# A two-layer hybrid trunk: conv taps split between TensorE and VectorE, a new split of the start's sums and dots, a packed dt product

## Chip, cores and metric

One core of one Trainium2 chip. The time is the device time of one execution in microseconds (us); the kernel's time is the median of several runs.

## What is computed

The reference is a two-layer trunk on x of shape (1, 512, 1024) in f32, conditioned by a vector c. Each layer is a mixer and a gated feed-forward network (FFN), each behind an RMSNorm with a shift and a scale that come from c. Cut to what the change touches:

```python
silu_c = silu(c)
for i in range(2):
    sh_m, sc_m, g_m, sh_f, sc_f, g_f = split(silu_c @ w_mod[i] + b_mod[i], 6)
    h = rmsnorm(x, norm_mix[i]) * (1 + sc_m) + sh_m
    y = even_mixer(h) if i == 0 else ssd_mixer(h)
    x = x + g_m * y
    h = rmsnorm(x, norm_ffn[i]) * (1 + sc_f) + sh_f
    x = x + g_f * conv_ffn(h)
return rmsnorm(x, final_norm)

# even_mixer: attention beside a conformer branch
a, g = split(conf_in, 2)                    # 512 channels each
h = causal_dwconv(a * sigmoid(g), conv_w, conv_b)   # 31 taps, per channel
h = silu(layernorm(h))
# ssd_mixer: z, xbc, dt = split(h @ w_in); dt has 32 columns
dt = softplus(dt + dt_bias)
```

## The kernel before, in words

Channels lie on the 128 partitions, tokens (512) along the free axis. Everything is in the function `trunk`: `even_layer` is layer 0's mixer, `odd_layer` layer 1's, `ffn` is called for both layers. The weights come from HBM in tiles of 128x1024 on SyncE's queue (L304); ScalarE rounds each tile to its high part (L312), VectorE takes the low part (L317), and a product is three matmuls per tile of 128 rows (`mm3`: L365 high by high, L366 high weight by low data, L367 low weight by high data).

The order of the work is made by a list-scheduling planner (`Plan`). A task has an engine, a cost, the tasks that it needs and the buffers that it takes and gives back; at each step the planner takes the ready task of the highest rank, and a table of numbers (MIXER0 for layer 0's mixer, MIXER1 for layer 1's) adds to the ranks. The order on TensorE (PE), ScalarE (ACT), VectorE (DVE) and GpSimd (POOL) is what the planner emits. SIDE tasks are the DMAs on GpSimd's queue, DMA tasks those on SyncE's (SP).

**Start.** x is loaded in eight tiles of 128 channels. ACT squares each (L672), PE sums the squares over the channels by matmuls against a vector of ones (L679: four 128x1 matmuls a tile, 32 in all). `warm` (L651) issues matmuls whose result is not used: two of 256 columns ahead of the sums, two behind them, three behind the spread of the norm factor. The shift and the scale of each 128 channels are dot products of silu(c) with 1024 weights, on DVE (`mod_dot`, L571: 128x1024, one for the scale and one for the shift of each of eight tiles kt). With them a tile's normalised data are split into high and low (L741, L745, L749), and TensorE adds this tile's part to six PSUM tiles at once (L753): the six first column blocks, which are the conv branch's a and g for three channel tiles. `finish` makes their last part with L365 to L367.

**Conv.** For each of four channel tiles i: ACT's sigmoid (L865), DVE's gate (L869, the result is `us[i]`), a store to an HBM row buffer with 30 zeros ahead (L872, on GpSimd's queue), and four fetches (L886, on GpSimd's queue, 270 KB each) that bring 32 channels each with four shifts, one in each block of 32 partitions. DVE makes the diagonal tap matrices (L877). `conv_product` (L893) runs 8 steps of 4 taps with 32 output channels per matmul: 32 matmuls a channel tile, 128 in all (31 taps, the 32nd is zero). ACT adds the bias from PSUM (L898), and PE forms the layer norm's mean (L1119) from the four results.

**dt.** In the odd layer `dt_in` makes the 32 dt columns by `mm3` (24 matmuls with 32 output rows), ACT copies them, and four transposes (L1393) turn them to tokens.

Of the kernel before, what the change touches and what calls it, by code (L numbers as in the profile page):

```python
# [21 lines left out]
ALU = mybir.AluOpType  # L22
# [12 lines left out]
CTAPS, CQ = 4, 8  # L35
# [4 lines left out]
_VEC = [("bmod", 96), ("nmix", 16), ("nffn", 16), ("fnorm", 8), ("bin", 14), ("ccw", 128), ("eye", 32),  # L40
# [29 lines left out]
WARM = (2, 2, 3)  # L70
# [3 lines left out]
MIXER1 = {'xdt': 122, 'differ': 108, 'square': 109, 'y_h': 85, 'join': 108, 'c4': 150, 'load': 91, 'weigh': -66, 'residual': -66, 'sums': -89, 'in': -132, 'osq': 53, 'head': 31, 'decay': 57, 'tokens': 114, 'state_in': -136, 'gate': 80, 'bt': -29, 'rows': 52, 'square_add': -7, 'root': 1, 'c4silu': 4, 'cbm': 34, 'newton': 45, 'out': -40, 'fetch': 95, 'c4tap': 135, 'yt': -82, 'pairs': -93, 'off': -50, 'turn': 75, 'rest': -66, 'skip': 99, 'osq_add': 62, 'diag': -21, 'dt': 123, 'norm': 0, 'z': -111, 'y_l': -149, 'carried': 11, 'free': -21, 'fetch_e': -26, 'grow': -23, 'state': 114, 'scan 2': -50, 'out 2': -150, 'scan 1': 76, 'in 2': -16, 'in 3': 2, 'in 0': 15, 'scan 3': -61, 'in 1': -150, 'out 3': -6, 'scan 0': 150, 'out 0': -35, 'out 1': -146, 'scr': 18}  # L74
N_XS, N_M, N_E = 8, 2, 2
N_S = 26
MIXER0 = {'sigmoid': 15, 'square': -70, 'osq_add': 86, 'head': -45, 'tap0': -113, 'attn_h': -71, 'conv_h': -27, 'out_c': -40, 'gated': 150, 'rest': -137, 'values': -27, 'rope': 53, 'rstd': -97, 'mod_sum': 7, 'attn_l': 150, 'var': -22, 'turn': 88, 'mod_end': 26, 'exp': 1, 'bring': 62, 'conv_sum': 54, 'out_a': 82, 'osq': -46, 'mod_act': -104, 'mod_add': 39, 'mod_free': 120, 'normalize': 121, 'load': -111, 'product': -139, 'mean_row': -71, 'mod_dve': 105, 'tap': -30, 'recip': 112, 'ln': 150, 'centre': -43, 'residual': -146, 'maxima': 21, 'rstd_row': -129, 'conv_l': 77, 'mean': 47, 'rope_in': 71, 'v_bias': -85, 'mod_load': -125, 'mod_dot': -93, 'root': 30, 'rows': 93, 'rows_in': 1, 'v_turn': -35, 'v_in': 112, 'mod 2': -75, 'head 0': 122, 'mu': 0, 'keys': 80, 'conv 0': 87, 'head 1': 90, 'mod 1': -108, 'head 3': -8, 'shifts': 58, 'scores': -52, 'mod 0': -50, 'conv 3': -51, 'conv 2': 119, 'cbias': 86, 'conv': 83, 'store': -26, 'taps': 96, 'conv 1': 150, 'head 2': 19, 'wg_load': -29, 'c_row': 8, 'norm': 51, 'hl': 8, 'x_newton': 150, 'preload': 31, 'others': -49, 'wg_head': 6, 'finish': 39, 'sines': 34, 'v_load': 121, 'first 4': 119, 'upper': 9, 'wg_rest': -15, 'hh': 130, 's_gain': -108, 'first 2': 100, 'widen': 150, 'x_load': -105, 'x_root': 57, 'x_add': -93, 'x_total': -33, 's_dot': 50, 'lh': 13, 'x_sq': -105, 'masks': -88, 't_turn': 29, 'c_in': -115, 'ss_load': -6, 'first 5': -3, 'gain': 23, 'w_free': -15, 'normed': 130, 'margins': -107, 'side': -45, 'x_row': -13, 'first 0': 29, 'h_dot': 103, 't_in': 26, 'first 1': -51, 'first 6': 29, 'angles': -108, 'first 3': 40, 'lower': 98, 'first 7': 52, 'h_bias': -80, 'x_sum': 24}
# [145 lines left out]
def trunk(ctx: ExitStack, tc: tile.TileContext, xT_d, vecs_d, rows_d, dsk_d, pos_d, const_d, wss_d, wg0_d,  # L223
# [397 lines left out]
    def even_layer(lp, cp, dp0):  # L621
# [26 lines left out]
        def warm(n):  # L648

            for _ in range(n):  # L650
                mm(g0[NG0 - 1][:, 0:2 * P], lhsT=ident, rhs=con[:, :2 * P], start=True, stop=True)  # L651
# [21 lines left out]

        def x_sum(k):
            if k == 0:
                st["xt"] = bank((P, NCH))
                warm(WARM[0])
# [3 lines left out]
            if k == KT - 1:  # L681
                warm(WARM[1])

        sums = None
        for k in range(KT):
            t = add("x_sq", "ACT", 0.62, lambda k=k: x_square(k), [xs_[k]], dict(tmp=1))
            sums = add("x_sum", "PE", 0.9, lambda k=k: x_sum(k), [t, sums, *cbs], dict(ps=1) if k == 0 else None, dict(tmp=1))
# [16 lines left out]
        def x_row():  # L704
            st["rb"] = spread(st["xr"])
            warm(WARM[2])
# [3 lines left out]
        rb_ = add("x_row", "PE", 2.1, x_row, [t], dict(ps=1))  # L710
# [24 lines left out]
        def shift(kt):  # L735
            S = modv[:, 0, kt:kt + 1]
            act(S, S, AF.Identity, bias=bm[:, 0, kt:kt + 1])
# [136 lines left out]
        def conv_taps(i):  # L874

            t_ = mod_raw().rearrange("p (n c) -> p n c", c=32)
            tt(t_, vec("eye", 0, 32).unsqueeze(1).broadcast_to([P, 32, 32]),  # L877
               vec("ccw", 32 * i, 32).unsqueeze(2).broadcast_to([P, 32, 32]), ALU.mult)
            st["cw", i] = t_.rearrange("p (g q) c -> p g q c", g=4)

        def conv_fetch(i):
# [3 lines left out]
            for g in range(4):  # L885
                nc.gpsimd.dma_start(u4[g], bass.AP(src.tensor, src.offset + 32 * g * CROW,  # L886
# [15 lines left out]
        def conv_tasks(i, after, pa, pg):  # L902
# [3 lines left out]
            d_ = plan.add("taps", "DVE", 1.3, lambda: conv_taps(i), [a_], dict(mr=1))  # L906
            c_ = plan.add("store", "SIDE", 1.0, lambda: conv_store(i), [b_])
            c_ = plan.add("shifts", "SIDE", 3.6, lambda: conv_fetch(i), [c_, margins_], dict(u4=1))
            c_ = plan.add("conv", "PE", 7.4, lambda: conv_product(i), [c_, d_], dict(ps=1), dict(mr=1, u4=1))
            conv_done[i] = plan.add("cbias", "ACT", 0.69, lambda: conv_bias(i), [c_], None, dict(ps=1))  # L910
# [423 lines left out]
    def odd_layer(lp, dp, start, after):  # L1334
# [17 lines left out]
        dwh, dwl = tmp((P, KT, 32), F32R), tmp((P, KT, 32), F32R)  # L1352
        split(wraw, dwh, dwl)
# [27 lines left out]
        def dt_in():  # L1381
            st["dtf"] = bank()
            for kt in range(KT):
                mm3(st["dtf"][0:32, :], (dwh[:, kt, :], dwl[:, kt, :]), *hn[kt], kt == 0, kt == KT - 1)

        def dt_copy():
            st["dts"] = tmp()
            nc.scalar.copy(st["dts"][0:32, :], st["dtf"][0:32, :])
# [58 lines left out]
        t = plan.add("dt", "PE", 5.2, dt_in, [], dict(ps=1))  # L1447
# [349 lines left out]
def pack(i):  # L1797
# [22 lines left out]
    r["wss"] = np.stack([wm[0][1], wm[0][0]], axis=1)  # L1820
    r["wmod"] = np.concatenate([wm[w // 6][w % 6] for w in MOD_ORDER])
# [15 lines left out]
    for g in range(4):  # L1837
# [6 lines left out]
    cw = np.zeros((CTAPS * CQ, 512), np.float32)  # L1844
    cw[:31] = a["conf_conv_w"][0]
# [4 lines left out]
        "ccw": cw.reshape(CQ, CTAPS, 4, 4, 32).transpose(1, 4, 2, 3, 0).reshape(P, P),  # L1850
# [37 lines left out]
```

## Time and profile before

| What | us |
|---|---|
| Median of three runs | 1365.77 (1363.56 to 1369.64) |
| Profiled execution, own time | 1364.35 |
| Its span in the trace | 1362.5 |
| PE busy | 1335.4 (98%) |
| DVE busy | 852.4 (63%) |
| ACT busy | 590.5 (43%) |
| POOL busy | 95.7 (7%) |

The profiled execution stands 1.42 us under the median. Its stages, in us from the start of the span: the start up to 57 (where `finish` begins), the products for the fourth channel tile up to 72, the conv from 72.05 to 118.4, attention and the mixer's output to about 238, FFN 0 to 620, the odd layer to 980, FFN 1 to 1340, the last norm to 1362.5. The busy share of TensorE is high in all of them, so the views that matter are the ones by stage.

### The profile page before, as it was taken

The numbers are of one execution on the slowest core, as the hardware profiler recorded it, in microseconds if no ns is written. First come the engines' busy times: TensorE is split into PE (matmuls) and PEld (weight loads), VectorE is DVE, ScalarE is ACT, GpSimd is POOL, SyncE is SP. The second block draws the span as 40 slices with busy tenths as digits, with TensorE's granted clock in tenths as the row PEclk, the third lists the DMA queues.
The fourth block names the chain that finished last, engine by engine and source line by source line (L and its number), as shares of the span: only waits on it lengthen the run. The fifth ranks groups of instructions, "written<-read, shape, count | busy, mean of one in ns | idle before, by whom it ended". The sixth has DMA issues, their size and how long they took to land.

```text
span 1362.5 us, 17553 instructions
## 1 busy us (share of the span) xinstructions
PE 1335.4 (98%) x6878; PEld 1093.9 (80%) x6879; DVE 852.4 (63%) x1316; ACT 590.5 (43%) x938; POOL 95.7 (7%) x173
## 2 busy tenths in 40 slices
PE   8979999999999999999999999999999999999997
PEld 7726778988888888898887887878898888888886
DVE  5912898786576567667588684788665434444443
ACT  4512763543233223246686762765354313322333
POOL 5420110000000000010010100110000000000001
PEclk7989999999999999999999999999999999999998
DMA  9595453475565565322552432432223233223311
GB/s 333 194 191 129 138 194 118 140 232 172 183 210 168 183 214 191 105 89 67 153 169 79 156 93 80 139 126 79 76 78 111 90 100 107 92 89 108 100 55 63
DMA packets 58212, 183.71 MB, mean 135 GB/s; under 512 B 10064, under 2 KB 13200, under 8 KB 58128
## 3 DMA queue, kind: packets, MB, share of 16 engines
q1 hardware_dynamic: 45184, 152.24, 35.2%
q0 software_dynamic: 12256, 29.69, 7.5%
q8 instruction: 54, 0.88, 0.3%
q10 hardware_dynamic: 688, 0.66, 0.2%
q14 instruction: 30, 0.25, 0.1%
HBM read 179.26 MB, written 3.28 MB: 134 GB/s over the span
## 4 chain that ended last, share of the span: by engine, by line
PE 87%; DMA 4%; DVE 3%; issue 2%; ACT 2%; POOL 1%; DVEq 0%; ACTq 0%; POOLq 0%
PE ps L365 26%; PE ps L367 26%; PE ps L366 26%; DMA s<-uc 2%; PE ps L893 2%; DMA M<-scr 2%; PE ps L399 1%; PE ps L391 1%; PE ps L1573 1%; PE ps L679 1%; ACT M L1523 1%; PE ps L1565 1%; PE ps L1551 1%; DVE mr L571 1%; PE ps L1041 0%
## 5 line engine op out<-in xcount | busy, mean ns | idle before, releaser
L365 PE MATMUL ps<-hn,wh 128*128 128x512 f32 (+1 forms) x1214 | 460.1, 379 | 0.8 <-ACT hn L441 0.8
L366 PE MATMUL ps<-hn,wh 128*128 128x512 f32 (+1 forms) x1214 | 454.1, 374 | 0.4
L367 PE MATMUL ps<-hn,wl 128*128 128x512 f32 (+1 forms) x1214 | 454.0, 374 | 0.0
L317 DVE TENSOR_TENSOR wl<-raw,wh 128x1024 fp32r<-128x1024 f32 (+1 forms) x208 | 250.8, 1209 | 144.4 <-ACT wh L312 143.4
L312 ACT CAST wh<-raw 128x1024 fp32r<-128x1024 f32 (+1 forms) x208 | 213.1, 1028 | 219.2 <-PE ps L366 209.9
L365 PEld LDWEIGHTS ps<-hn,wh 128*128 128x128 f32 x1214 | 228.6, 188 | 43.0 <-issue 1.7
L366 PEld LDWEIGHTS ps<-hn,wh 128*128 128x128 f32 x1214 | 228.7, 188 | 42.0 <-issue 1.4
L367 PEld LDWEIGHTS ps<-hn,wl 128*128 128x128 f32 x1214 | 228.5, 188 | 41.0
L454 DVE SCALAR_TENSOR_TENSOR x<-ps,modv,x 128x512 f32<-128x512 f32 (+1 forms) x108 | 73.7, 689 | 119.6 <-PE ps L367 119.4
L365 PE MATMUL ps<-fh,wh 128*128 128x512 f32 (+1 forms) x380 | 142.2, 374 | 0.0
L366 PE MATMUL ps<-fl,wh 128*128 128x512 f32 (+1 forms) x380 | 141.9, 373 | 0.0
L367 PE MATMUL ps<-fh,wl 128*128 128x512 f32 (+1 forms) x380 | 141.9, 373 | 0.0
L571 DVE SCALAR_TENSOR_TENSOR mr<-mr,cb 128x1024 f32<-128x1024 f32 x96 | 116.1, 1218 | 3.5 <-DMA mr<-in_wss_dram 2.2
L1281 ACT ACTIVATE tmp<-ps,vecs 128x512 f32<-128x512 f32 x44 | 34.3, 780 | 115.4 <-PE ps L367 115.4
L1282 DVE SCALAR_TENSOR_TENSOR tmp<-ps,vecs,tmp 128x511 f32<-128x511 f32 x44 | 32.9, 748 | 80.0 <-ACT tmp L1281 80.0
L366 PEld LDWEIGHTS ps<-fl,wh 128*128 128x128 f32 x380 | 71.5, 188 | 12.8
L365 PEld LDWEIGHTS ps<-fh,wh 128*128 128x128 f32 x380 | 71.5, 188 | 12.6
L367 PEld LDWEIGHTS ps<-fh,wl 128*128 128x128 f32 x380 | 71.5, 188 | 12.6
L429 POOL TENSOR_TENSOR ssq<-ssq,tmp 128x512 f32<-128x512 f32 x10 | 13.4, 1338 | 805.1 <-ACT tmp L428 805.1
L290 ACT CAST fh<-tmp 128x512 fp32r<-128x512 f32 x44 | 27.3, 620 | 96.4 <-DVE tmp L1286 96.4
L1284 ACT ACTIVATE tmp<-tmp 128x512 f32<-128x512 f32 x44 | 27.8, 633 | 74.9 <-DVE tmp L1283 74.9
L291 DVE TENSOR_TENSOR fl<-tmp,fh 128x512 fp32r<-128x512 f32 x44 | 30.5, 693 | 30.2 <-ACT fh L290 30.2
(277 smaller groups left out, 1500.0 us busy)
## 6 DMA issues: line engine op xcount, KB each, us to landing
raw<-in_w_dram SPq DMA_DIRECT2D x176, 512.0 KB, 3.7
mr<-in_wmod_dram SPq DMA_DIRECT2D x56, 512.0 KB, 3.6
raw<-in_w_dram SPq DMA_DIRECT2D x32, 448.0 KB, 3.3
mr<-in_wmod_dram POOLq DMA_DIRECT2D x24, 512.0 KB, 5.1
mr<-in_wss_dram SPq DMA_DIRECT2D x16, 512.0 KB, 6.2
M<-scr POOLq DMA_DIRECT2D x16, 512.0 KB, 4.7
s<-uc POOLq DMA_DIRECT2D x16, 270.0 KB, 15.1
raw<-in_wg_dram SPq DMA_DIRECT2D x8, 384.0 KB, 5.7
```

The lines of the kernel that those rows point to most:

```text
L290: nc.scalar.copy(h, src)
L291: (eng or nc.vector).tensor_tensor(l, src, h.bitcast(F32), ALU.subtract)
L312: nc.scalar.copy(h, self.raw[i].rearrange("p (k m) -> p k m", m=P))
L317: eng.tensor_tensor(l, self.raw[i].rearrange("p (k m) -> p k m", m=P), h.bitcast(F32), ALU.subtract)
L365: mm(ps, lhsT=w[0], rhs=ah, start=first, stop=False)
L366: mm(ps, lhsT=w[0], rhs=al, start=False, stop=False)
L367: mm(ps, lhsT=w[1], rhs=ah, start=False, stop=last)
L454: stt(x[:, m, hs], ps, gate(m), x[:, m, hs], ALU.mult, ALU.add)
L571: stt(raw, raw, 1.0, mod_pool[2], ALU.mult, ALU.mult, accum_out=out)
L1281: act(c, pg, AF.Identity, bias=vec("fcb", i), scale=vec("fcw", 3 * i + 2))
L1282: stt(c[:, 1:], pg[:, :T - 1], vec("fcw", 3 * i + 1), c[:, 1:], ALU.mult, ALU.add)
L1284: act(c, c, AF.Silu)
```

## The change

- **Square sums.** DVE adds the squares of tiles 1 to 5 onto tile 0's (`x_add`, five operations); PE sums that one, tile 6 and tile 7 (12 matmuls of 128x1 instead of 32).
- **Fillers.** The 256-column fillers at three fixed places become 16 tasks of one 128-column matmul each, which the planner places.
- **Shift dots.** For kt below 4 the shift's dot is made on PE (`pe_dot`: 8 f32 matmuls of 32x128 in four column groups; ACT copies the 128x128 result, `pe_in`; one matmul adds its rows, `pe_sum`). The host lays these weights out by row. DVE keeps the other four shift dots and all eight scale dots.
- **Conv.** PE makes 24 taps (CQ 8 to 6; 24 matmuls a channel tile). The last seven taps are made from `us[i]` directly: ACT makes the first with the bias (`late_first`, in place of the bias from PSUM), DVE the other six (`late_tap`, 128x506 to 128x511), and DVE adds the PSUM result (`conv_sum`). The fetches go to SyncE's queue.
- **dt.** The high and the low weights lie side by side, so that one matmul with 64 output rows makes high by high and low by high: 16 matmuls instead of 24. The four transposes become four matmuls against an identity of two blocks, which adds the halves.
- **Order.** MIXER0 and MIXER1 have new numbers.

```diff
-CTAPS, CQ = 4, 8
+CTAPS, CQ = 4, 6
+NLATE = 31 - CTAPS * CQ
-WARM = (2, 2, 3)
+WARM = 16
+PE_DOTS = 4
-MIXER0 = {'sigmoid': 15, 'square': -70, ...}
+MIXER0 = {'sigmoid': 33, 'square': -70, ...}
...
-                mm(g0[NG0 - 1][:, 0:2 * P], lhsT=ident, rhs=con[:, :2 * P], start=True, stop=True)
+            mm(g0[NG0 - 1][:, 0:P], lhsT=ident, rhs=con[:, :P], start=True, stop=True)
...
+        def x_add(k):
+            tt(st["xq", 0], st["xq", 0], st["xq", k], ALU.add)
...
+            elif k < KT - 2:
+                sums = add("x_add", "DVE", 0.69, lambda k=k: x_add(k), [t, sums], None, dict(tmp=1))
...
+        def pe_dot(kt):
+            o = st["pd", kt] = bank((P, 2 * P))
+            for n in range(0, KT, 4):
+                for g in range(4):
+                    k = n + g
+                    mm(o[32 * g:32 * g + 32, 0:P], lhsT=cond[:, k:k + 1].broadcast_to([P, 32]),
+                       rhs=st["ss", kt, 1][:, k * P:(k + 1) * P], start=(n == 0), stop=(n > 0), tile_position=(0, 32 * g))
+        def pe_in(kt):
+            st["pi", kt] = tmp((P, P))
+            nc.scalar.copy(st["pi", kt], st["pd", kt][:, 0:P])
+        def pe_sum(kt):
+            mm(st["pd", kt][:, P:P + 1], lhsT=st["pi", kt], rhs=vec("eye", 0, 1), start=True, stop=True)
...
-                nc.gpsimd.dma_start(u4[g], bass.AP(src.tensor, src.offset + 32 * g * CROW,
+                nc.sync.dma_start(u4[g], bass.AP(src.tensor, src.offset + 32 * g * CROW,
...
-        def conv_bias(i):
+        def late_first(i):
             cv[i] = tile_s()
-            act(cv[i], st["co", i], AF.Identity, bias=vec("ccb", i))
+            act(cv[i], us[i], AF.Identity, bias=vec("ccb", i), scale=vec("cct", NLATE * i + NLATE - 1))
+        def late_tap(i, d):
+            stt(cv[i][:, d:], us[i][:, :T - d], vec("cct", NLATE * i + NLATE - 1 - d), cv[i][:, d:], ALU.mult, ALU.add)
+        def conv_sum(i):
+            tt(cv[i], st["co", i], cv[i], ALU.add)
...
-                mm3(st["dtf"][0:32, :], (dwh[:, kt, :], dwl[:, kt, :]), *hn[kt], kt == 0, kt == KT - 1)
+                if kt:
+                    mm(o[0:32, :], lhsT=dw[:, kt, 0:32], rhs=hn[kt][1], start=False, stop=False)
+                mm(o[0:64, :], lhsT=dw[:, kt, :], rhs=hn[kt][0], start=(kt == 0), stop=(kt == KT - 1))
...
-                nc.tensor.transpose(st["dps"][:, c, :], st["dts"][0:32, c * P:(c + 1) * P], ident[0:32, 0:32])
+                mm(st["dps"][:, c, :], lhsT=st["dts"][0:64, c * P:(c + 1) * P], rhs=vec("eye", 0, 32)[0:64, :], start=True, stop=True)
```

How the instructions move is seen at three places. The first is TensorE at the start, before the first products; `con` holds the constants, `tmp` the squares, L651 is the filler and L679 a tile's square sums. Before:

```order
L399 MATMUL ps_198<-con 128x128 x4
L651 MATMUL ps_180<-con 128x256 x2
L679 MATMUL ps_212<-ones,tmp_193 128x1 x4
...
L679 MATMUL ps_212<-ones,tmp_238 128x1 x4
L651 MATMUL ps_180<-con 128x256 x2
L399 MATMUL ps_299<-con,sm_292 128x128 x4
L651 MATMUL ps_180<-con 128x256 x3
L753 MATMUL ps_175<-hn_322,wh_268 128x512
```

Now (L652 is the filler, L682 the sums, L755 a shift dot's matmuls and L763 its row sum, L779 the first product):

```order
L401 MATMUL ps_198<-con 128x128 x4
L652 MATMUL ps_180<-con 128x128 x8
L682 MATMUL ps_243<-ones,tmp_193 128x1 x4
L652 MATMUL ps_180<-con 128x128
L682 MATMUL ps_243<-ones,tmp_228 128x1 x4
L755 MATMUL ps_260<-mr_223,con 32x128 x8
L682 MATMUL ps_243<-ones,tmp_232 128x1 x4
L763 MATMUL ps_260<-vecs,tmp_273 128x1
L652 MATMUL ps_180<-con 128x128 x5
L401 MATMUL ps_305<-con,sm_296 128x128 x4
L652 MATMUL ps_180<-con 128x128 x2
L755 MATMUL ps_320<-mr_253,con 32x128 x8
```

Eight rows of sums became three, the first shift dot stands ahead of the last sum, the second ahead of the first product; the other two stand among the products.

The second place is the queue of the conv's fetches (`uc` are the row buffers in HBM, `s` the fetched tiles, `mr` and `raw` weight loads). Before, on GpSimd:

```order
L872 DMA uc_108<-s_653 128x512
L872 DMA uc_109<-s_684 128x512
L872 DMA uc_110<-s_690 128x512
L886 DMA s_704<-uc_108 128x1x540
...
L886 DMA s_746<-uc_109 128x1x540
L872 DMA uc_111<-s_792 128x512
L886 DMA s_839<-uc_110 128x1x540
...
L886 DMA s_887<-uc_111 128x1x540
L563 DMA mr_1148<-in_wmod_dram 128x1024
```

Now, on SyncE (the stores stay on GpSimd, as L903):

```order
L306 DMA raw_678<-in_w_dram 128x1024
L306 DMA raw_689<-in_w_dram 128x1024
L919 DMA s_743<-uc_108 128x1x532
...
L919 DMA s_791<-uc_109 128x1x532
L919 DMA s_866<-uc_110 128x1x532
...
L919 DMA s_914<-uc_111 128x1x532
L306 DMA raw_882<-in_w_dram 128x1024
L306 DMA raw_925<-in_w_dram 128x1024
```

All sixteen fetches stand in one row with no weight load between them; the next weight load stands behind the last of them, in the same queue.

The third place is VectorE during the conv (L900 is the gate, L910 the tap matrices, L935 a late tap, L938 the add of the PSUM result, L319 the low part of a weight tile, L975 the first step of the rotary embedding that follows). Now:

```order
L900 SCALAR_TENSOR_TENSOR s_833<-ps_695,vecs,tmp_826 128x512
L935 SCALAR_TENSOR_TENSOR s_728<-s_693,vecs,s_728 128x508
L910 TENSOR_TENSOR mr_839<-vecs 128x768
L935 SCALAR_TENSOR_TENSOR s_728<-s_693,vecs,s_728 128x507
L935 SCALAR_TENSOR_TENSOR s_836<-s_833,vecs,s_836 128x511
L935 SCALAR_TENSOR_TENSOR s_728<-s_693,vecs,s_728 128x506
L935 SCALAR_TENSOR_TENSOR s_836<-s_833,vecs,s_836 128x510
L938 TENSOR_TENSOR s_728<-ps_801,s_728 128x512
...
L319 TENSOR_TENSOR wl_721<-raw_654,wh_720 128x1024
...
L938 TENSOR_TENSOR s_836<-ps_933,s_836 128x512
L319 TENSOR_TENSOR wl_995<-raw_930,wh_994 128x1024
```

The 24 late taps and four adds stand between the gates and the low parts of the weights of the products that follow; before, this stretch held the four gates, the four tap matrices and six low parts, and nothing else.

## Rows read from the trace of the kernel before

**Rows 1.** Windows by stage: engines' busy us, granted PE clock, DMA share, GB/s.

```profile
core 0: us, PE busy (x) PEld busy (x) DVE busy (x) ACT busy (x) POOL busy (x), PEclk, DMA share, GB/s
0.00:240.00 240.00, 224.25 (x1322) 165.37 (x1323) 155.69 (x300) 106.43 (x213) 53.61 (x111) 0.94 0.61 184
240.00:620.00 380.00, 379.85 (x1860) 322.33 (x1861) 254.27 (x382) 134.06 (x182) 6.89 (x5) 1.00 0.53 169
620.00:980.00 360.00, 358.51 (x1908) 291.51 (x1907) 262.51 (x386) 218.42 (x364) 25.86 (x48) 1.00 0.36 113
```

**Rows 2.** Windows within the first stage, the same columns.

```profile
11.30:20.40 9.10, 9.10 (x45) 9.10 (x44) 3.45 (x5) 2.70 (x5) 7.70 (x20) 0.50 1.03 410
25.00:60.90 35.90, 35.10 (x156) 27.86 (x156) 33.91 (x59) 21.04 (x36) 9.59 (x18) 1.00 0.64 222
76.00:86.40 10.40, 7.28 (x30) 1.57 (x34) 2.45 (x2) 2.09 (x2) 2.04 (x3) 0.51 1.07 213
86.40:94.70 8.30, 5.37 (x40) 1.09 (x32) 0.00 (x0) 0.69 (x1) 0.00 (x0) 1.00 1.02 226
94.70:118.40 23.70, 23.70 (x191) 10.57 (x192) 0.00 (x0) 2.06 (x3) 6.00 (x10) 1.00 0.78 182
```

**Rows 3.** Chain of waits, first 125 us: start us, us, what.

```profile
9.09 11.35 PE ps L679 x64
...
25.80 2.29 DVE mr L571 x4
...
69.58 25.09 DMA s<-uc
...
94.70 13.92 PE ps L893 x122
108.62 1.05 PE ps L1119 x2
109.68 7.63 PE ps L893 x64
...
118.37 0.23 PE ps L365
```

**Rows 4.** Waits of PE: total us, times, longest us.

```profile
PE ps L893 <- DMA s<-uc: 7.9, 5, 2.7
...
PE ps L391 <- DVE sz L1600: 1.0, 1, 1.0
```

**Rows 5.** PE timeline, start of the conv: start us, us, instruction.

```profile
72.05 1.05 PE L893 MATMUL ps<-s,mr 128*32 128x512 f32 x2
```

**Rows 6.** POOL timeline in the conv: issues of fetches, with the idle time before.

```profile
64.80 5.45 POOL L886 DMA_DIRECT2D s<-uc  x8 [1.21 <-DMA uc<-s]
...
96.51 2.68 POOL L886 DMA_DIRECT2D s<-uc  x4 [10.79 <-DMA uc<-s]
```

**Rows 7.** DMA issues, 60 to 120 us: KB each, median us to landing.

```profile
s<-uc POOLq DMA_DIRECT2D x16, 270.0 KB, 15.1
```

**Rows 8.** PE timeline among the first products: a 128-column pass, what follows, and `finish`'s first.

```profile
47.90 0.60 PE L836 MATMUL ps<-con,s 128*128 128x128 f32 x4
48.25 1.64 PE L753 MATMUL ps<-hn,wl 128*128 128x512 f32 x6
...
57.00 0.39 PE L365 MATMUL ps<-hn,wh 128*128 128x512 f32 x1
```

**Rows 9.** Groups of DVE by shape, 0 to 240 us: busy us, mean ns, idle before.

```profile
L571 DVE SCALAR_TENSOR_TENSOR mr<-mr,cb 128x1024 f32<-128x1024 f32 x40 | 48.0, 1220 | 3.5 <-DMA mr<-in_wss_dram 2.2 <-DMA mr<-in_wmod_dram 1.2
...
L877 DVE TENSOR_TENSOR mr<-vecs 128x1024 f32<-128x1024 f32 x4 | 4.7, 1216 | 0.0
...
L1063 DVE TENSOR_TENSOR s<-ps,s 128x512 f32<-128x512 f32 x4 | 2.7, 687 | 0.9 <-PE ps L1041 0.9
...
L1149 DVE SCALAR_TENSOR_TENSOR s<-s,vecs,ps 128x512 f32<-128x512 f32 x4 | 2.7, 744 | 0.0
```

**Rows 10.** DVE timeline around the conv's end, with the idle time before.

```profile
124.74 1.22 DVE L317 TENSOR_TENSOR wl<-raw,wh 128x1024 fp32r<-128x1024 f32 x1 [41.43 <-ACT wh L312]
```

More of the change, by code (lines that the diff above doesn't have):

```diff
@@ new lines @@
+MIXER0 = {'sigmoid': 33, 'square': -70, 'osq_add': 86, 'head': -45, 'tap0': -113, 'attn_h': -71, 'conv_h': 4, 'out_c': -40, 'gated': 144, 'rest': -137, 'values': -27, 'rope': 19, 'rstd': -97, 'mod_sum': 7, 'attn_l': 150, 'var': -22, 'turn': 85, 'mod_end': 61, 'exp': -12, 'bring': 62, 'conv_sum': 54, 'out_a': 82, 'osq': -46, 'mod_act': -104, 'mod_add': 39, 'mod_free': 120, 'normalize': 121, 'load': -149, 'product': -146, 'mean_row': -71, 'mod_dve': 105, 'tap': -30, 'recip': 112, 'ln': 150, 'centre': -43, 'residual': -146, 'maxima': 21, 'rstd_row': -129, 'conv_l': 77, 'mean': 47, 'rope_in': 71, 'v_bias': -86, 'mod_load': -125, 'mod_dot': -93, 'root': 21, 'rows': 93, 'rows_in': -24, 'v_turn': -35, 'v_in': 112, 'mod 2': -49, 'head 0': 122, 'mu': 0, 'keys': 80, 'conv 0': 87, 'head 1': 90, 'mod 1': -108, 'head 3': -47, 'shifts': 40, 'scores': -52, 'mod 0': -50, 'conv 3': -51, 'conv 2': 119, 'cbias': 86, 'conv': 83, 'store': -26, 'taps': 0, 'conv 1': 150, 'head 2': 19, 'wg_load': -107, 'c_row': 150, 'norm': 51, 'hl': 8, 'x_newton': 150, 'preload': 31, 'others': -49, 'wg_head': -12, 'finish': 16, 'sines': 34, 'v_load': 121, 'first 4': 119, 'upper': 9, 'wg_rest': -15, 'hh': 130, 's_gain': -108, 'first 2': -60, 'widen': -135, 'x_load': -105, 'x_root': 150, 'x_add': 150, 'x_total': -33, 's_dot': 51, 'lh': -117, 'x_sq': 150, 'masks': -88, 't_turn': 29, 'c_in': 150, 'ss_load': -2, 'first 5': -65, 'gain': 0, 'w_free': -15, 'normed': 130, 'margins': -107, 'side': -78, 'x_row': 150, 'first 0': 29, 'h_dot': 107, 't_in': -4, 'first 1': -19, 'first 6': 29, 'angles': -108, 'first 3': 40, 'lower': 98, 'first 7': 86, 'h_bias': -80, 'x_sum': 150, 'late': 23, 'late0': 139, 'csum': 110, 'warm': -150, 'p_dot': -150, 'p_in': 50, 'p_sum': 50}
@@ L646, in even_layer, with warm @@
         add = plan.add
-        def warm(n):
-            for _ in range(n):
-                mm(g0[NG0 - 1][:, 0:2 * P], lhsT=ident, rhs=con[:, :2 * P], start=True, stop=True)
+        def warm():
+            mm(g0[NG0 - 1][:, 0:P], lhsT=ident, rhs=con[:, :P], start=True, stop=True)
         plan.group = "norm"
@@ L686, in even_layer @@
             t = add("x_sq", "ACT", 0.62, lambda k=k: x_square(k), [xs_[k]], dict(tmp=1))
-            sums = add("x_sum", "PE", 0.9, lambda k=k: x_sum(k), [t, sums, *cbs], dict(ps=1) if k == 0 else None, dict(tmp=1))
+            if k == 0:
+                sums = t
+            elif k < KT - 2:
+                sums = add("x_add", "DVE", 0.69, lambda k=k: x_add(k), [t, sums], None, dict(tmp=1))
+            else:
+                if k == KT - 2:
+                    sums = add("x_sum", "PE", 1.0, lambda: x_sum(0), [sums], dict(ps=1), dict(tmp=1))
+                sums = add("x_sum", "PE", 1.0, lambda k=k: x_sum(k), [t, sums], None, dict(tmp=1))
+        for _ in range(WARM):
+            add("warm", "PE", 0.45, warm, cbs)
         table_ = add("preload", "ACT", 0.2, lambda: act(small(1), eps[:, 0:1], AF.Sqrt), [t], table="sqrt")
@@ L905, in conv_tasks @@
             b_ = plan.add("gated", "DVE", 0.69, lambda: gated(i, pa), [a_], None, dict(ps=2, tmp=1))
[L906 to L910, printed above, removed]
+            d_ = plan.add("taps", "DVE", 0.95, lambda: conv_taps(i), [a_], dict(mr=1))
+            e_ = plan.add("late0", "ACT", 0.69, lambda: late_first(i), [b_])
+            for d in range(1, NLATE):
+                e_ = plan.add("late", "DVE", 0.69, lambda d=d: late_tap(i, d), [e_])
+            c_ = plan.add("store", "SIDE", 1.5, lambda: conv_store(i), [b_])
+            c_ = plan.add("shifts", "DMA", 3.6, lambda: conv_fetch(i), [c_, margins_], dict(u4=1))
+            c_ = plan.add("conv", "PE", 1.0 * CQ, lambda: conv_product(i), [c_, d_], dict(ps=1), dict(mr=1, u4=1))
+            conv_done[i] = plan.add("csum", "DVE", 0.69, lambda: conv_sum(i), [c_, e_], None, dict(ps=1))
         for i in range(3):
```

48 lines of the change are left out of this document (27 added, 21 removed).

## The prediction

> **What bounds the kernel now.** I read the windows by stage first: TensorE (PE) is busy for 224.25 of the first 240 us, 379.85 of the next 380 and 358.51 of the 360 of the odd layer [rows 1]. In a stage with PE full, time is won only by work taken off PE; the first 240 us are the only long stretch with something else to win, some 16 us of idle time and a granted clock of 0.94. The windows inside it [rows 2] show where. From 11.3 to 20.4 us PE runs at half clock (0.50). From 25 to 60.9 us it is full (35.10 of 35.90) and VectorE (DVE) nearly so (33.91). From 76 to 94.7 us it is busy for 7.28 + 5.37 of 18.7 us, the first 10.4 of them at 0.51, while the DMA engines are full (share 1.07 and 1.02) at 213 to 226 GB/s; from 94.7 to 118.4 us it is full again. The chain of waits [rows 3] names the same: the square sums (11.35 us), then DVE's dots, then a fetch of the conv's shifted copies for 25.09 us up to the matmul at 94.70. The waits of PE [rows 4] put 7.9 us on these fetches, and 1.0 us on the largest in the odd layer. So three places count: the start, the conv from 72.05 us [rows 5] to 118.37 us [rows 3], and dt. I call the start of `finish`, 57.0 us before [rows 8], F.
>
> **Start: taken as 0.** The 32 sums take 11.35 us at half clock, 0.355 us each; 12 remain, so up to 20 x 0.355 = 7.1 us leaves the path. Against that stand four shift dots on PE. No row shows a 32x128 f32 matmul in column groups. The nearest from above is a plain 128-column one: four matmul rows from 47.90 to 48.25 us, 0.35 / 4 = 0.09 us a row [rows 8], and an f32 matmul has two rows, so 16 x 0.09 = 1.4 us a dot. From below, the conv's passes of 512 columns follow each other in 7.63 / 64 = 0.119 us [rows 3], so 128 columns in a quarter of that: 16 x 0.03 = 0.5 us. I take 0.8 us, between them, and 2.4 us for the three dots that do not stand between the sums. The first dot stands ahead of the last sum and, at half clock, takes 1 to 2.8 us of what the sums give. DVE loses four dots of 1.22 us [rows 9] and gains five adds of 0.69. The first products then still wait for scale dots on DVE, which stand in the chain behind 25.80 us [rows 3]; so I let the first product come only 1 to 2 us earlier, and as the stage behind it is full on PE, 2.4 us of added dots take that back: net 0. The ends: 7.1 us gained less 3 x 0.5 = 1.5, so 5.6 faster; nothing gained and 3 x 1.4 = 4.2 us added. The fillers are work that is not used, and PE waits where they stand.
>
> [...]
>
> **Conv: -21.7 us.** Before, 46.3 us (72.05 to 118.37). The undisturbed pace is 13.92 us for 122 rows, 0.114, and 7.63 for 64, 0.119 [rows 3]; I take 0.117. 96 matmuls are 192 rows: 22.5 us, and the two mean operations on the path 2.1: 24.6 us. Gain 21.7. Of that, 64 rows x 0.117 = 7.5 us is work taken away; the other 14.2 us is the waits for fetches and the half clock that followed them. It goes only if the fetches come in time.
>
> Do they? Before, GpSimd issued eight fetches from 64.80 us (F+7.8), and the eighth landed at 94.66: 30 us, 3.7 us each; median 15.1 us from issue to landing [rows 7]. They shared the DMA engines with weight loads on SyncE's queue, and the next four were issued only at 96.51 us [rows 6]. Bytes are the measure: 270 KB at 213 to 226 GB/s [rows 2] is 1.2 to 1.27 us a fetch, 20 us for sixteen. Now no weight load stands between them. Issued from F+7.8, the four of the first conv land at about F+13 and PE comes to it at F+15, as before; each conv needs 5.65 us of PE and 5.1 us of fetches, so PE stays behind. The last must land by F+33.3 (conv end F+39.6, less 1.05 and 45 rows): 25.5 us for sixteen, 1.6 us each. A fetch of the fourth conv waits for tiles that the first conv frees (F+21), and 4 x 1.27 more is F+26. Behind the fetches on SyncE's queue wait weight loads; the tiles loaded ahead cover the products that follow.
>
> DVE takes 24 late taps of about 0.67 us (a 512-column operation of this kind is four in 2.7 us [rows 9]) and four adds of 0.69: 18.9 us. The tap matrices shrink from 1.22 to some 0.91 us. Before, DVE idled 41.43 us to 124.74 us [rows 10], that is F+26.3 to F+67.7. All of the new list from the first gate on is 18.9 + 4 x 0.75 (gates) + 4 x 0.91 + 6 x 1.22 (low parts) = 32.9 us; the stores that precede the fetches follow the gates, so it begins some us ahead of F+7.8; from F+5 it ends near F+38, while PE needs its last sum behind the last conv and a product, after F+40. So it is covered, by little; without cover each us counts. ScalarE's first tap takes the place of its bias pass, one for one.
>
> **dt: -1.8 us.** Eight matmuls of 0.23 us (the pitch of a 512-column matmul at 118.37 us [rows 3]) leave a full PE: 1.8 us. The four token matmuls and the copy keep their number.
>
> **Order.** The new numbers shift the odd layer's work; its 360 us hold 1.5 us in which PE is idle [rows 1], and a new order may lose as much: 0, within 2 us each way.
>
> **Sum.** 0 - 21.7 - 1.8 = -23.5. From the profiled 1364.35 us that is 1340.9, say 1341. The median of 1365.77 stands 1.4 above the profiled time; about 0.5% (6.8 us) is what a measurement of this kernel can tell from no change.
>
> **Rivals.**
>
> *The queue does not matter (0.15).* The fetches could keep their pace, because the DMA engines were full whoever issued. The first eight at 3.7 us, the next at 1.9 (eight in the 15 us to 109.68): the last lands at F+7.8+30+15 = F+52.8, then 45 rows and a mean: F+59.1, against F+61.4 before. Gain 2.3 + 1.8: 1360. At 1.9 us for all sixteen the last lands at F+38.2, the conv ends at F+44.6: gain 16.8 + 1.8, 1346. For it: the share over 1. Against: half the bytes then moving were weights, which now stand behind. I give 1360 a chance of 0.06 and 1346 one of 0.09. [...]
>
> *The start gains (0.14).* If the first products come as early as the sums allow, 5.6 us more: 1335.
>
> *VectorE becomes the bound (0.04): slower.* The 18.9 us of taps and adds would stand on the path. This happens if DVE comes to them only when the fetches end, so that PE's means wait for sums and the low parts of the next weights come behind them; it decides when DVE's list ends later than F+60, where the conv ended before. Then 18.9 us less the 7.5 taken off PE and 1.8 of dt, with the 14.2 us of waits kept: +9.6, 1374. Against: the 41 us of idle time, and gates that are ready by F+5.
>
> *The odd layer's new order stalls (0.03).* Every us there is PE's; 10 us would give 1351, and more than 23.5 us are needed to lose all. PE is idle there for 1.5 us now, so stalls of that size would be new.
>
> That the change does not do what it says is excluded by the order of instructions, where the taps and fetches stand in their new places.
>
> **How the numbers follow.** Forecast 0.64, start 0.14, 1346 0.09, 1360 0.06, VectorE 0.04, odd layer 0.03. The range: from 1335 take 4 us for the part of the start and the order that I can't price, 1331; above, the start's 4.2 and the order's 2 on 1341 and the slower pace on 1346, with 5 us for a clock that drops again (10.4 us at 0.51 [rows 2] cost half of it), 1352. Outside lie 1360, VectorE and parts of the others: some 0.15. Faster by over 0.5% (under 1359): 0.64 + 0.14 + 0.09 + 0.03 = 0.90, within 0.5%: 0.06 and a little, 0.07; slower 0.03, VectorE's part beyond the bound.
>
> **What would show it.** Right: PE's conv rows follow without a wait for fetches, at full clock, some 24.6 us from the first to the mean; DVE's idle stretch is filled with taps; the wait for L919's fetches is near 0; `dt` shows 16 rows. Wrong: PE waiting at the conv for `s<-uc` (first rival), PE's means waiting for DVE (third), new waits in the odd layer; `finish` well before F = 55 or after 59 would tell the start's part.

## The result: slower by 1%

The changed kernel takes 1382.21 us in the median of 4 runs (1380.72 to 1383.12), the kernel before 1365.51 (4 runs, 1363.56 to 1369.64): a ratio of 1.0109, interval 1.0084 to 1.0135 (the quotient of the medians is 1.0122, inside it). The forecast of 1341 and its range, 1331 to 1352, are both missed, on the other side of no change. The profiled execution of the change has a span of 1381.2 us, 18.7 more than before.

### Profile after

The waits of PE, the first rows (us in total, times, longest), where [rows 4] stood before:

```profile
PE ps L926 <- DMA s<-uc: 18.7, 10, 3.2
...
PE ps L369 <- DVE wl L319: 3.0, 2, 2.2
```

The wait for the conv's fetches (L926 is the conv's matmul now) has grown from 7.9 us to 18.7, though each conv has a quarter fewer matmuls. (That the span grew by 18.7 us too is chance.) The PE timeline of the conv (start us, us, instruction, idle time before):

```profile
71.72 1.04 PE L926 MATMUL ps<-s,mr 128*32 128x512 f32 x2
73.63 1.04 PE L926 MATMUL ps<-s,mr 128*32 128x512 f32 x2 [0.87 <-DMA s<-uc]
76.41 1.04 PE L926 MATMUL ps<-s,mr 128*32 128x512 f32 x2 [1.73 <-DMA s<-uc]
79.17 7.10 PE L926 MATMUL ps<-s,mr 128*32 128x512 f32 x44 [1.71 <-DMA s<-uc]
88.50 1.21 PE L926 MATMUL ps<-s,mr 128*32 128x512 f32 x2 [2.23 <-DMA s<-uc]
92.92 1.92 PE L926 MATMUL ps<-s,mr 128*32 128x512 f32 x2 [3.22 <-DMA s<-uc]
...
119.90 1.89 PE L926 MATMUL ps<-s,mr 128*32 128x512 f32 x2 [2.19 <-DMA s<-uc]
123.95 6.73 PE L926 MATMUL ps<-s,mr 128*32 128x512 f32 x42 [2.16 <-DMA s<-uc]
130.61 1.12 PE L1162 MATMUL ps<-s,ones 128*128 128x512 f32 x2
```

PE starts the conv as early as before (71.72 against 72.05 [rows 5]) and then, at each of these waits, gets one fetched tile every 2 to 4 us, to the last conv. SyncE's queue in the same stretch:

```profile
64.02 44.24 SPq L919 DMA_DIRECT2D s<-uc  x16
108.36 21.27 SPq L306 DMA_DIRECT2D raw<-in_w_dram  x5
```

These rows are the issuing. The sixteen fetches hold the queue for 44.24 us, 2.8 each, and the weight loads stand behind them. The last fetched tile reaches PE only at 123.95 us, 60 us after the first issue: 3.7 us a fetch over all. While fetches run alone they arrive 2.8 us apart (PE at 73.63, 76.41, 79.17); where other loads run too, they are up to 4.4 us apart (88.50 to 92.92). A window of the change in which only fetches run (columns as in [rows 1]):

```profile
96.00:104.00 8.00, 7.03 (x46) 1.64 (x46) 0.94 (x2) 0.00 (x0) 0.54 (x1) 0.78 0.26 101
```

This is the row that matters. PE waits for transfers, and the DMA engines are not full but three quarters idle: a share of 0.26 at 101 GB/s, where before, with weights moving beside the fetches, they were full at 213 to 226 [rows 2]. Of 16 engines 0.26 is 4.2, and four is the outermost dimension of the fetch's source, `[[1, CTAPS], [CROW, 32], [1, CWIN]]`: four shifts of 32 rows. That the one follows from the other, four engines for a source with four outermost, is my estimate from this share, and the theory that the runs test. The trace also records packets, each with its start and its duration: from 96 to 104 us 4.2 packets of fetches (2128 bytes each) are in flight on the mean and 6 at most, and 7 at most in the whole conv, while five to six fetches are issued and have not landed. Which engine carries a packet the trace does not say. Before, fetches of this shape stood on GpSimd's queue; the packets of the first run below show the difference.

VectorE is not the cause. Its timeline in the change:

```profile
86.14 0.69 DVE L938 TENSOR_TENSOR s<-ps,s 128x512 f32<-128x512 f32 x1 [6.55 <-PE ps L926]
...
103.06 0.69 DVE L938 TENSOR_TENSOR s<-ps,s 128x512 f32<-128x512 f32 x1 [13.78 <-PE ps L926]
```

It waits 6.55 and 13.78 us for PE's conv.

PE's waits of 18.7 us are half of what the conv loses: from its first row to the start of the next product it takes 59.5 us, and 22.5 with the fetch reordered (the second experiment). The clock adds to them. The granted clock is 0.77 on the mean over that stretch (71.72 to 131.17 us), which is 27.3 us at 0.50 and the rest at 1.00; before it was 0.89 (72.05 to 118.37 us), 10.2 us at 0.50, and with the fetch reordered, where PE did not wait, 1.00. In the change it fell behind waits: it was 1.00 from 71.70 to 79.00 us, with PE idle for 0.87, 1.73 and 1.71 us up to 79.17, and 0.50 from 79.00 to 82.40.

Where the 18.7 us of the span lie, read from the first or last instruction of the same work in the traces (us; "shape mended" is the change with the fetch reordered, the second experiment):

| Stretch | Before | Change | Shape mended |
|---|---|---|---|
| Start to the conv's first matmul | 72.0 | 71.7 | 70.7 |
| Conv to the last mean | 58.5 | 72.1 | 35.1 |
| To the first FFN's first convolution | 128.8 | 131.5 | 132.1 |
| To the dt token matmuls | 375.3 | 373.5 | 373.4 |
| To the second FFN's last convolution | 670.3 | 672.8 | 672.1 |
| To the end | 57.6 | 59.6 | 59.5 |

The conv alone makes 13.6 of the 18.7.

### The profile page after: what moved, and what is told of

It is laid out like the page before. It is cut to its first block, busy times and chain, and to the rows that moved or that the text cites. A ratio compares the mean times of both kernels' runs of the same rounds, so it can differ in the third digit from the quotient of the medians.

```text
span 1381.2 us, 17566 instructions
## 1 busy us (share of the span) xinstructions
PE 1334.8 (97%) x6860; PEld 1087.6 (79%) x6861; DVE 868.1 (63%) x1341; ACT 594.5 (43%) x945; POOL 84.5 (6%) x157
## 4 chain that ended last, share of the span: by engine, by line
PE 78%; issue 11%; DVE 4%; DMA 3%; ACT 3%; POOL 1%; POOLq 0%; DVEq 0%; ACTq 0%
PE ps L367 24%; PE ps L368 24%; PE ps L369 24%; DMA M<-scr 2%; ACT M L1571 1%; PE ps L401 1%; PE ps L393 1%; PE ps L1599 1%; DVE s L935 1%; PE ps L1621 1%; PE ps L779 1%; DMA mr<-in_wss_dram 1%; POOL mr L565 1%; PE ps L1587 1%; DMA mr<-in_wmod_dram 0%
## 5 line engine op out<-in xcount | busy, mean ns | idle before, releaser
L319 DVE TENSOR_TENSOR wl<-raw,wh 128x1024 fp32r<-128x1024 f32 (+1 forms) x208 | 251.1, 1209 | 112.5 <-ACT wh L314 109.9
L573 DVE SCALAR_TENSOR_TENSOR mr<-mr,cb 128x1024 f32<-128x1024 f32 x92 | 111.4, 1218 | 4.6 <-DMA mr<-in_wmod_dram 3.2
L292 ACT CAST fh<-tmp 128x512 fp32r<-128x512 f32 x44 | 27.3, 620 | 96.2 <-DVE tmp L1329 96.2
L926 PE MATMUL ps<-s,mr 128*32 128x512 f32 x192 | 39.2, 776 | 18.7 <-DMA s<-uc 18.7
```

Source lines behind the costliest of these rows:

```text
L292: nc.scalar.copy(h, src)
L319: eng.tensor_tensor(l, self.raw[i].rearrange("p (k m) -> p k m", m=P), h.bitcast(F32), ALU.subtract)
L573: stt(raw, raw, 1.0, mod_pool[2], ALU.mult, ALU.mult, accum_out=out)
L926: mm(o[32 * g:32 * g + 32, :], lhsT=st["cw", i][:, g, n, :], rhs=st["u4", i][g][:, 4 * n:4 * n + T], start=(n == 0), stop=(n == CQ - 1), t ...
```

## The experiments

Ratios are against the kernel before, run beside each on the same chip. The first four runs share a chip, on which the kernel before took 1364.67 us. The change with GpSimd's queue and channels outermost, and the parts from the odd layer's numbers to the shift dots, ran on a second (1365.57); the kernel before with channels outermost on GpSimd's queue, dt and all old numbers on a third (1369.94); the last run on a fourth (1365.03). Between chips the ratio is what can be compared.

### Which part of the fetch: queue or shape

**Fetches back on GpSimd's queue.**

```diff
-                nc.sync.dma_start(u4[g], bass.AP(src.tensor, ...
+                nc.gpsimd.dma_start(u4[g], bass.AP(src.tensor, ...
...
-            c_ = plan.add("shifts", "DMA", 3.6, ...
+            c_ = plan.add("shifts", "SIDE", 3.6, ...
```

> The change with the conv's fetches back on GpSimd's queue, the rest kept. Theory (a fetch whose source's outermost dimension is 4, the four shifts, runs through only 4 of the 16 DMA engines when SyncE's queue issues it: the trace of the change shows a DMA share of 0.21 to 0.26 at 84 to 101 GB/s while only fetches run): GpSimd's fetches fill all 16 engines as before, share over 0.8, conv ended 20 to 30 us earlier than in the change: 1350 to 1362 us. Rival (VectorE's late taps are the bound): no change, 1380 to 1384. Rival (the new order of the odd layer and of attention cost most of the loss): 1375 to 1382.

1367.47 us, ratio 1.0014 (0.9994 to 1.0034). Better than the change by 15 us, as the theory said in direction, but above its range: PE still waits 13.1 us for fetches. PE, ScalarE and VectorE keep the order of the change, so VectorE's taps and the new order are out as the main cause. But the queue of before with this shape is not good either.

The packets tell the two queues apart. At the start of the conv, with no other load running, those in flight climb by fours as more fetches are issued: 4 from 65.0 to 66.0 us, 8 from 66.75 to 68.0, then 12, and 16 from 70.25. The trace of before has the same steps: 4.0 on the mean from 66.3 to 67.5 us and 8.1 from 68.0 to 69.5. So a fetch of this shape seems to have four packets in flight on GpSimd's queue too, but there several fetches add up, where on SyncE's queue all of them together had 4.2.

**On SyncE's queue, channels outermost.** The partitions hold channel by shift instead of shift by channel; the tap weights and the identity (`eyc`) are laid out to match. No instruction moves.

```diff
-            tt(t_, vec("eye", 0, 32)...
+            tt(t_, vec("eyc", 0, 32)...
...
-    [[1, CTAPS], [CROW, 32], [1, CWIN]]
+    [[CROW, 32], [1, CTAPS], [1, CWIN]]
...
-        "ccw": cw[:CTAPS * CQ]....transpose(1, 4, 2, 3, 0)...
+        "ccw": cw[:CTAPS * CQ]....transpose(4, 1, 2, 3, 0)...
...
+        "eyc": np.repeat(np.eye(32, dtype=np.float32), CTAPS, axis=0),
```

> The change with the fetches still on SyncE's queue, but each fetch's source with 32 channels outermost and the four shifts inside (the tap matrices' rows and the weights reordered to match): same order of instructions on every engine, same bytes, same row lengths. Theory (outermost dimension 4 means 4 DMA engines): 16 engines, a fetch in 1.2 to 1.6 us, waits for fetches under 3 us instead of 18.7, 1340 to 1352 us. Rival (SyncE's queue handles these fetches one after the other, whatever their shape): no change, 1380 to 1384. Rival (late taps or the new order): no change.

1346.02 us, ratio 0.9858 (0.9833 to 0.9883): 36 us below the change, in the theory's range; the rivals that foresaw no change fall. Its SyncE queue, one window, and its PE timeline:

```profile
62.14 17.38 SPq L919 DMA_DIRECT2D s<-uc  x16
```

```profile
80.00:90.00 10.00, 10.00 (x90) 2.85 (x86) 6.08 (x8) 1.04 (x1) 1.08 (x2) 1.00 1.02 398
```

```profile
70.70 15.66 PE L926 MATMUL ps<-s,mr 128*32 128x512 f32 x144
...
87.34 5.36 PE L926 MATMUL ps<-s,mr 128*32 128x512 f32 x48
```

SyncE issues the sixteen fetches in 17.38 us instead of 44.24, the engines are full (a share of 1.02) at 398 GB/s, and 192 PE rows run without one wait and at full clock. A packet takes the same 87 ns (median) as in the change, but from 68 to 72 us 15.6 are in flight on the mean, where the change has 4.2 from 96 to 104 us. Same bytes, same queue, same order: the shape was the cause, by the number of packets in flight.

**The kernel before with the queue alone, and with queue and shape.**

```diff
-                nc.gpsimd.dma_start(u4[g], bass.AP(src.tensor, ...
+                nc.sync.dma_start(u4[g], bass.AP(src.tensor, ...
...
-            c_ = plan.add("shifts", "SIDE", 3.6, ...
+            c_ = plan.add("shifts", "DMA", 3.6, ...
```

> The kernel before with only the fetches moved to SyncE's queue (same shape, shifts outermost). Theory (4 engines): 2.75 us a fetch, sixteen in 44 us from F+8, with weight loads between: conv ended at F+58 to F+75, where it was F+61 before: 1364 to 1380 us. Rival (late taps or order cost the loss, the queue is harmless or good): 1345 to 1362 us.

1388.49 us, ratio 1.0174 (1.0143 to 1.0205): slower than the theory's range. PE waits 18.7 us for the fetches, as in the change, and the last eight are issued only from 103.52 us, behind five weight loads. A window with hardly anything but fetches:

```profile
112.00:120.00 8.00, 3.82 (x4) 0.37 (x4) 0.00 (x0) 0.00 (x0) 0.00 (x0) 0.50 0.26 100
```

The share of 0.26 at 100 GB/s again, without any other part of the change. The same kernel with channels outermost:

> The kernel before with the fetches on SyncE's queue and 32 channels outermost in the source. Theory (16 engines): most of the 14 us of fetch waits and half clock goes: 1349 to 1358 us. Rival (SyncE's queue is slow for these fetches in any shape): as the run with the shifts outermost.

1356.02 us, ratio 0.9931 (0.9905 to 0.9957), as the theory said; PE waits 1.7 us.

**GpSimd's queue with channels outermost,** in the change and in the kernel before. The edits are the first two diffs above, taken together, and the second alone (in the kernel before `eye` itself is reordered).

> The change with the fetches on GpSimd's queue and 32 channels outermost in the source. Theory (the shape matters only for the number of engines that SyncE's queue uses; GpSimd's fetches already keep all 16 busy, but at half the bytes per busy time, 213 GB/s against 400 for SyncE's with channels outermost): as the change on GpSimd's queue with shifts outermost, 1362 to 1370 us. Rival (channels outermost also makes each transfer cheaper, so the queue doesn't matter any more): 1345 to 1354 us.

1347.72 us, ratio 0.9864 (0.9844 to 0.9884). The theory fails here and the rival holds: the shape makes GpSimd's fetches cheap too (4.6 us from issue to landing in the median, 12.8 in the first run).

> The kernel before with one thing changed: the fetches stay on GpSimd's queue, but 32 channels are outermost in their source (the order of instructions is the same on every engine). Theory (the shape is what counts: on SyncE's queue the shifts outermost leave 4 engines, on GpSimd's they make twice the packets, and with channels outermost either queue is fast): the waits of PE for fetches fall from 7.9 us to under 2, 1352 to 1358 us, as the kernel before with channels outermost on SyncE's queue (1356.0). Rival (the kernel before needs the queue too, because weight loads and fetches meet in the engines): 1361 to 1366 us.

1352.87 us, ratio 0.9881 (0.9861 to 0.9901). With every instruction in its old place, one reordered access pattern makes the kernel before faster by 1.2%, and more than on SyncE's queue (0.9931). Its conv has no wait (first line), and a fetch lands 6.0 us after its issue (second) instead of 15.1 [rows 7]:

```profile
72.12 21.28 PE L893 MATMUL ps<-s,mr 128*32 128x512 f32 x192
```

```profile
s<-uc POOLq DMA_DIRECT2D x16, 270.0 KB, 6.0
```

The DMA views of 60 to 120 us, before and then with channels outermost:

```profile
DMA packets 6363, 11.66 MB, mean 194 GB/s; under 512 B 3584, under 2 KB 3584, under 8 KB 6361
```

```profile
DMA packets 3544, 12.56 MB, mean 209 GB/s; under 512 B 544, under 2 KB 544, under 8 KB 3541
```

On GpSimd's queue the shifts outermost go with 3040 more packets under 512 B, 190 a fetch; with channels outermost these are gone and slices of the window reach over 400 GB/s, where [rows 2] show 213 to 226. The small packets themselves are not the cost: they are of 8 bytes and 9 ns each, 36 us in all over 16 engines. The data packets are the same in both shapes, 1024 of 4320 bytes, but take 337 ns on the mean with the shifts outermost and 193 with the channels; the other loads' packets of 4096 bytes beside them (66 to 90 us) take 282 ns instead of 159 in the median. So with the shifts outermost the packets in flight go by fours on either queue: on SyncE's there were 4.2 for all fetches, on GpSimd's up to 16, but there the packets are slower. Why they are slower stays open.

### The other parts, on the version with channels outermost on SyncE's queue

**The odd layer's numbers as before** (`MIXER1` of the kernel before).

> The change with channels outermost on SyncE's queue, and the odd layer's table of numbers (MIXER1) as before. In the profiles the stretch from the dt token matmuls to the last convolution of the second FFN took 670.3, 669.9 and 670.6 us with the old numbers and 672.8, 672.6 and 672.1 with the new. Theory (the new order stalls by about 2 us): 1343 to 1345 us. Rival (the difference is noise or follows from what came ahead): 1346 us, the stretch 672.

1345.45 us, ratio 0.9848 (0.9831 to 0.9865); its stretch took 671.8 us. The theory of 2 us is not borne out: the change and its three versions with another fetch have 672.1 to 672.8, so this order costs 0.3 to 1.0.

**All taps on PE.**

```diff
-CTAPS, CQ = 4, 6
-NLATE = 31 - CTAPS * CQ
+CTAPS, CQ = 4, 8
+NLATE = 0
...
-            act(cv[i], us[i], AF.Identity, bias=vec("ccb", i), scale=...
+            act(cv[i], st["co", i], AF.Identity, bias=vec("ccb", i))
...
-            e_ = plan.add("late0", "ACT", 0.69, lambda: late_first(i), [b_])
-            for d in range(1, NLATE):
-                e_ = plan.add("late", "DVE", 0.69, lambda d=d: late_tap(i, d), [e_])
...
-            conv_done[i] = plan.add("csum", "DVE", 0.69, lambda: conv_sum(i), ...
+            conv_done[i] = plan.add("cbias", "ACT", 0.69, lambda: late_first(i), ...
```

> The change with channels outermost on SyncE's queue, but all 32 taps on TensorE, no late taps on VectorE, and the bias from PSUM as before (the planner places the tasks anew). Theory (VectorE's taps are hidden, so the 64 rows of PE are what they save): 7 to 8 us more, 1353 to 1355 us. Rival (the taps delay the weights' low parts and the attention that follow and give back half or more): 1346 to 1350 us.

1362.14 us, ratio 0.9976 (0.996 to 0.9992): 16 us more than with the late taps, twice what the theory expected and far above the rival. The planner placed the mixer's work anew, conv matmuls now run to 149 us, and a new wait stands in attention:

```profile
PE ps L1081 <- ACT s L1070: 6.3, 1, 6.3
```

```profile
160.00:180.00 20.00, 13.62 (x90) 10.48 (x91) 12.93 (x30) 12.66 (x26) 1.62 (x3) 0.67 0.14 46
```

The clock is 0.67 there. So the run tells what taps and a plan that was not made for them cost together. The taps alone are seen by the conv stretches of two runs whose order is the same there: 42.5 us in the kernel before with channels outermost (72.1 to 114.6), 35.1 here: 7.4 us for 64 rows.

**All shift dots on VectorE** (`PE_DOTS = 0`).

> The change with channels outermost on SyncE's queue, with all shift dots on VectorE again (PE_DOTS 0; the square sums as in the change). Theory (the four dots with their row sums take 3 us of a full PE and give VectorE the same back, net 0): 1344.5 to 1347.5 us, first product earlier or later by at most 1 us. Rival (VectorE set the pace of the start and the dots bought 3 us or more): 1349 us or more.

1358.9 us, ratio 0.9952 (0.9936 to 0.9967): the rival's side. PE's waits in it hold two that the version with the dots has almost none of:

```profile
PE ps L779 <- ACT hn L771: 2.7, 2, 1.4
...
PE ps L779 <- DVE hn L775: 2.1, 1, 2.1
```

The last product of the start begins at 58.7 us instead of 55.4: 3.3 us there, PE's work on the dots included. The size is loose: nine traces with the dots have it between 55.0 and 57.1. The rest cannot be put down to the dots. The whole trace is 17.1 us longer than that of the shape mended. The conv starts 8.7 us later, but behind one more product (24 matmuls). The stretch from the last mean to the first FFN's convolution still takes 134.4 us instead of 132.1, and from the dt token matmuls to the second FFN's last convolution it takes 677.5 instead of 672.1, with every engine's instructions in the same order (PE waits 6.0 us in the odd layer instead of 2.4). So the total overstates the dots.

**dt as before.**

```diff
-        split(wraw, dw[:, :, 0:32], dw[:, :, 32:64])
+        split(wraw, dwh, dwl)
...
-                mm(o[0:64, :], lhsT=dw[:, kt, :], rhs=hn[kt][0], start=(kt == 0), stop=(kt == KT - 1))
+                mm3(st["dtf"][0:32, :], (dwh[:, kt, :], dwl[:, kt, :]), *hn[kt], kt == 0, kt == KT - 1)
...
-                mm(st["dps"][:, c, :], lhsT=st["dts"][0:64, c * P:(c + 1) * P], rhs=...
+                nc.tensor.transpose(st["dps"][:, c, :], st["dts"][0:32, c * P:(c + 1) * P], ident[0:32, 0:32])
```

> The change with channels outermost on SyncE's queue, and the dt product as before (24 matmuls and four transposes; the planner orders the odd layer with the new numbers). Theory (the packed product saves 8 x 0.23 = 1.8 us of PE, its f32 token matmuls take 0.65 us more, 1.01 against 0.36): 1346.5 to 1348.5 us. Rival (the odd layer waits on its chain of decays and gives all of it back): 1345 to 1346.5 us.

1347.38 us, ratio 0.9842 (0.982 to 0.9865), on another chip than the run that it would be held against; the intervals overlap, so the times do not decide. Its trace takes 375.3 us from the first FFN's first convolution to the token matmuls, as the kernel before does, where the packed product takes 373.4: 1.9 us gained. How much of that is left further on is open: between the first and the last convolution of the two FFNs it has 1046.4 us and the packed product 1045.5, but the change itself, with the same instructions there, has 1046.3. So what remains of the forecast 1.8 us is not separated from the spread of single traces.

**All old numbers** (in both tables, for the names that were there before).

> The change with channels outermost on SyncE's queue, and in both tables the numbers of before for all names that were there before (the names that the change adds keep theirs). From the last mean of the conv to the first convolution of the FFN the profiles show 128.8 to 130.1 us with the old numbers and no late taps, 131.5 to 132.1 with the change. Theory (the new order of the first layer's mixer costs these 2 to 3 us): 1342 to 1344 us. Rival (the late taps put the low parts of the weights behind them, and the order has no share): 1345 to 1347 us.

1343.33 us, ratio 0.9811 (0.9792 to 0.983), the fastest of all, in the theory's range; the run with dt as before, on the same chip and with the new numbers, took 4 us more. The stretch behind the conv takes 130.5 us. In the traces with the new numbers and late taps it takes 131.5 to 132.1, in four traces with the old numbers and no late taps 128.8 to 130.1. So 1.0 to 1.6 us are the order's; the wait for a weight's low part (2.2 us) is gone. What is left lies with the late taps or was not separated.

**Four more taps a channel tile on VectorE** (`CQ = 5`), on the version with the old numbers.

> The version with channels outermost and the old order numbers, with 20 taps on TensorE and 11 late ones (CQ 5 instead of 6): 32 PE rows of 0.11 us fewer, 16 more late taps of 0.67 us on VectorE (10.7 us). Theory (VectorE has about 11 idle us in 80 to 100 us, so the taps are still covered): 3.5 us less than with CQ 6, some 0.979 of the kernel before. Rival (the low parts of the weights and the last sums now come after PE needs them, VectorE becomes the bound): PE waits for low parts or sums, as long as with CQ 6 or longer, 0.981 to 0.99 of the kernel before.

1347.66 us, ratio 0.9872 (0.9853 to 0.9891): no gain, a number in the rival's range, but not for the rival's reason. PE's waits for low parts come to 1.0 us and it has none for the conv's sums; a fetch comes late:

```profile
88.40 8.80 PE L926 MATMUL ps<-s,mr 128*32 128x512 f32 x40 [4.59 <-DMA s<-uc]
```

With fewer rows PE is through the first three convs at 83.81 us, and the planner put the first mean behind the last conv (with 24 taps the last conv starts at 87.42, behind that mean). So PE comes to the last conv ahead of its fetches. Whether VectorE would cover the taps stays open.

## Why the prediction was wrong

**The step that failed** is the price of a fetch: "270 KB at 213 to 226 GB/s [rows 2] is 1.2 to 1.27 us a fetch". I took a rate seen with the DMA engines full on GpSimd's queue and carried it to SyncE's, as if bytes alone set it. There a fetch (266 KB now) measured 2.8 us while fetches ran alone, with 4.2 packets in flight for all of them, and 3.7 us on the mean of the sixteen. The condition that I wrote down myself (1.6 us each) was thus broken, and the last fetch came at F+67.3 (F is 56.7 us in the change) instead of before F+33.3.

The 2.8 us alone do not give the loss. By the prediction's own sum sixteen of them end at F+52.6 and the conv at F+58.9, still 2.5 us earlier than before: about 1360. Two more things had been taken at nothing. The fetches arrived further apart where other loads ran, which makes the 3.7. And the half clock, which was to go with the waits, grew with them, from 10.2 us to 27.3.

Two things should have warned: 213 GB/s with full engines is half of the 410 that the same engines moved at the start [rows 2], so these transfers were already odd; and the outermost dimension of the fetch's source is four, where a weight load has 128 rows, so no row had this shape on SyncE's queue. None could show 101 GB/s, but the bound from above belonged at several times the price, and with it the chance of a slower kernel.

**The rivals.** The first (the queue does not matter) pointed at the right transfer and had the wrong sign: with this shape the queue matters much, for the worse. Its worst price, 3.7 us for eight fetches, is what all sixteen took; it still ended at 1360, because it let the rest run at 1.9. The slower rival was VectorE's taps; in the conv VectorE waits for PE (6.55 and 13.78 us), not PE for it.

**The steps that held,** in the profile with the shape mended (1344.67 us against the 1340.9 of the sum; against 1364.35 before):

- Conv, -21.7: measured 58.5 to 35.1 up to the last mean, -23.4. The waits and the half clock went entirely, and 192 rows took 21 us (15.66 + 5.36) instead of 22.5.
- Start, 0: measured -1.3 (-0.3 in the change itself, which has the same start), within its ends. The dots gave VectorE more back than assumed, by the one trace without them; on PE each of the two at full clock takes 0.57 us from its first row to the next product's (30.56 and 34.35 us in the change), near the 0.5 that the sum has as the lower end, the switch to 32x128 matmuls and back included.
- VectorE's cover, "by little": it holds through the conv. Behind it 3.3 us were lost that the sum has at nothing; one wait of 2.2 us there, for the low part of a weight, is avoided by the older numbers.
- dt, -1.8: the stretch up to the token matmuls shortened by 1.9, but those are eight rows on PE now instead of four and take 1.01 us instead of 0.36. What remained over the layer is not separated.
- Order, 0: the mixer's cost 1.0 to 1.6 us, the odd layer's 0.3 to 1.0, together about the 2 us that were allowed.
- The end of the kernel took 57.6 us before and 59.5 here. It took 60.8 in the run of before with channels outermost on GpSimd's queue, which has the old order, so it varies between executions and belongs to no part.

The sum of the terms was right to 4 us for the kernel that I had in mind, in part because errors cancel: conv and start came 3 us better than priced, the stretch behind the conv, the odd layer with the second FFN, and the end 7 us worse. The forecast failed on one operation that changed its queue.

## What to carry to other kernels

Here a transfer's rate belonged to its queue and its access pattern together: with the shifts outermost 101 GB/s on SyncE's queue, with the channels outermost 398 on the same queue. When a DMA moves to another queue, price it from a row of the same shape on that queue, or leave a factor of several open. A PE that waited while the DMA share sat at 0.26 was here a matter of shape, not of bandwidth: one reordered access pattern was worth 36 us in the change and 1.2% in the kernel before. And a part that is switched off under a planner measures the new plan as well, so read its price from the stretch in the trace, not from the total.

## What was not expected of the hardware

The same fetch (266 to 270 KB) ran at three paces. With four shifts outermost on SyncE's queue it took 2.8 us with a DMA share of 0.26, and sixteen fetches in a queue never had more than 7 packets in flight. In the same shape on GpSimd's queue the packets in flight climbed by fours, to 16 with several fetches; the engines were full at 213 to 226 GB/s, with data packets of 337 ns on the mean. With 32 channels outermost it took about 1.1 us at 398 GB/s on SyncE's queue, and on GpSimd's the same data packets took 193 ns.
